# Seven block products in place of eight for three of eleven pairs of rows in the last output products of a two-layer decoder trunk

## The chip, the cores and the metric

The kernel runs on one core of one Trainium2 chip. The metric is the device time of one execution in microseconds; before the change the median of three runs is 2616.62 us.

## The reference

A decoder trunk of two layers on 256 tokens of width 2048, everything in fp32. Layer 0 mixes tokens by multi-scale retention, layer 1 by a short gated convolution; each layer then has a SwiGLU feed-forward part with 5632 inner rows. Every sub-layer is normed, scaled and shifted by columns that come from a conditioning vector `c` (the modulation), and its output is multiplied by a gate column and added to `x`. A final norm with a gain closes the trunk.

```python
def swiglu(h, w_in, w_out):
    a, b = jnp.split(h @ w_in, 2, axis=-1)
    return (jax.nn.silu(a) * b) @ w_out

for i in range(DEPTH):
    mod = (c_act @ w_mod[i] + b_mod[i])[:, None, :]
    sh1, sc1, g1, sh2, sc2, g2 = jnp.split(mod, 6, axis=-1)
    ...
    x = (x + g1 * y).astype(x.dtype)
    h = (rms_norm(x, norm2_g[i]) * (1.0 + sc2) + sh2).astype(x.dtype)
    x = (x + g2 * swiglu(h, ffn_w_in[i], ffn_w_out[i])).astype(x.dtype)
return rms_norm(x, final_g).astype(x.dtype)
```

## The kernel before

**Weights.** All weights lie in one array in the order of their use, cut into chunks of 128 x 2048 numbers (1 MB). `fetch` loads a chunk into one of three `raw` buffers from SP's queue. `prepare` works on half a chunk, a *piece* of 128 x 1024: ACT rounds it to `hi` (L311), VectorE subtracts to get the rest `lo` (L314). There are four buffers each of `hi` and `lo`. `take` hands out the block for the next matmul and sees to it that two more pieces are asked for (`AHEAD`). Activations are split in the same manner, and a product is the sum of three matmuls: hi with hi, hi with lo, lo with hi.

**Modulation.** Each column of the modulation is one load of 1 MB of `w_mod` into a `raw` buffer and one reduction on VectorE with `c` spread over 2048 columns (`cb`, L245), with a lowered priority. `paced` doles these out as weight blocks of 128 x 128 are used, after the table `plan_mod`; `needed` forces out the ones that a step cannot do without.

**The last layer's feed-forward part** goes in two halves of 22 inner rows (rows of 128). `swiglu_in` makes the 22 gate products of a half and splits each into `mid`. Beside the first half's, `turn` transposes `x` to one row for each token (`xt`). Then the output product: the moving operand is a weight block of 128 rows by 512 columns, the stationary one 128 tokens of `mid`, and the sum over 22 rows of each column block of 512 stands in two PSUM banks, one for each 128 tokens (`by_token`, L371 to L373). The four column blocks follow one another. `added` multiplies a sum by the gate (L1065) and adds it to `xt` (L1066); in the second half it also squares (L1069) and multiplies by the gain (L1071). For the last column block the final six rows (`TAIL_ROWS`) are done first for one half of the tokens, then for the other, so that `stored` can finish and store the first half meanwhile.

**Gate and gain.** `gate_stored` transposes the gate column to a row and stores it to DRAM, `spread` loads it back broadcast over 128 partitions into the space of `x` that is free by then, and the gain with it. Both are called within the first column block of the first half, before its rows 2 and 8 (`STORE_AT`, `LOAD_AT`).

TensorE's order is written out by hand; on VectorE, ACT and POOL a scheduler orders the instructions of this stage by priority. All loads and stores go through SP's queue, in order.

Of the kernel before, what the change touches and what calls it, by code (L numbers as in the profile page):

```python
# [17 lines left out]
P = 128  # L18
# [22 lines left out]
STORE_AT, LOAD_AT = 2, 8  # L41
# [14 lines left out]
class Group:  # L56


    def __init__(self, cols, width=P, ks=range(KT)):

        self.items = [c if isinstance(c, tuple) else (c, width) for c in cols]
        self.cols, self.ks = [c for c, _ in self.items], list(ks)
        self.n = sum(w for _, w in self.items) // P

# [67 lines left out]
LAST_OUT = [[Group([c], DV, ks=ks) for c in range(0, D, DV)] for ks in halves(DFF)]  # L132


def in_use_order():
# [10 lines left out]
    for layer in range(DEPTH):  # L146
# [5 lines left out]
        for part in range(2):  # L152
            for g in FFN_IN[part]:
                yield "ffn_w_in", layer, g
            for g in (LAST_OUT if layer == DEPTH - 1 else FFN_OUT)[part]:
                yield "ffn_w_out", layer, g


def laid_out(arrays):
# [4 lines left out]
    for key, i, g in in_use_order():  # L164
        for k in g.ks:
            for c, w in g.items:
                o = at % CHUNK
                out[at // CHUNK, :, o : o + w] = arrays[key][i, k * P : (k + 1) * P, c : c + w]
                at += w
# [18 lines left out]
def trunk(ctx: ExitStack, tc: tile.TileContext, x_in, c_in, pos_in, w_mod, cols_in, gain_in, tab_in, w_all, out):  # L188
# [20 lines left out]
    cb = const.tile([P, D], F32, tag="cb", name="cb")  # L209
    x4 = [const.tile([P, 4, S], F32, tag=f"x{i}", name=f"x{i}") for i in range(0, KT, 4)]  # L210
# [17 lines left out]
    nc.vector.memset(half, -0.5)  # L228

# [35 lines left out]
    plan_mod = [(early, 0), (1024, 18), (1984, 49), (5184, 9 * KT), (5888, n_mod)]  # L265
# [19 lines left out]
    order = [(g, k, c, w) for _, _, g in in_use_order() for k in g.ks for c, w in g.items]  # L285
    order.reverse()
    n_halves = w_all.shape[0] * CHUNK // HALF
    ready, taken_cols, raws, fetched, n_fetched = [], [0], [], [], [0]
# [7 lines left out]
    def prepare(between=None):  # L296
        n = prepared[0]
        if n == n_halves:
            return
        prepared[0] += 1  # L300
        i = n * HALF % CHUNK
        if i == 0:
# [5 lines left out]
        raw = raws[0][:, i : i + HALF]  # L308
        hi = wpool.tile([P, HALF], F32R, tag="hi", name=name("hi"))
        lo = wpool.tile([P, HALF], F32R, tag="lo", name=name("lo"))  # L310
# [4 lines left out]
        ready.append((hi, lo))  # L315

    prepared = [0]

    def take(group, k, col, width=P):

        assert order.pop() == (group, k, col, width)
        i = taken_cols[0] % HALF
        if i == 0:
            if ready and taken_cols[0]:
                ready.pop(0)
            while len(ready) < 1 + AHEAD * (units[0] >= first):
# [4 lines left out]
        taken_cols[0] += width  # L331
        return [t[:, i : i + width] for t in ready[0]]
# [32 lines left out]

    def by_token(banks, hi, lo, h, first, last, halves=range(2)):

        for t in halves:
            o = banks[t].rearrange("p a b -> p (a b)")
            ht = h[:, :, t * P : (t + 1) * P]  # L370
            nc.tensor.matmul(o, ht[:, 0, :], hi, start=first, stop=False)  # L371
            nc.tensor.matmul(o, ht[:, 0, :], lo, start=False, stop=False)  # L372
            nc.tensor.matmul(o, ht[:, 1, :], hi, start=False, stop=last)  # L373

    def packed(g, act, base=0, before=None, between=None, banks=None):
# [5 lines left out]
        for k in g.ks:  # L381
# [4 lines left out]
            for i, (c, width) in enumerate(g.items):  # L386
# [3 lines left out]
                if width == DV:  # L390
                    by_token(banks[at // 2 : at // 2 + 2], hi, lo, h, k == g.ks[0], k == g.ks[-1])
# [19 lines left out]
    def split(dst, src, at=slice(0, S)):  # L411
# [551 lines left out]
    def swiglu_in(layer, part, acc, mid, beside=()):  # L963

        pending, done, beside = [], 0, list(beside)
        for i, g in enumerate(FFN_IN[part]):
            pending += [sums(g)] if part or i else normed(acc, layer, 1, g)
            while len(pending) >= 2:
# [8 lines left out]
                split(mid[done], m)  # L977
# [55 lines left out]

    turns = [lambda t=t, c=c: turn(t, c) for c in range(4) for t in range(2)]


    flat = [v.rearrange("p a b -> p (a b)") for v in x4]
    gate_of = [at(flat[c // 2], c % 2) for c in range(4)]
    gain_of = [at(flat[2 + c // 2], c % 2) for c in range(4)]
# [10 lines left out]
    def spread():  # L1050
# [4 lines left out]
        for i in range(2):  # L1055
            o = slice(i * D // 2, (i + 1) * D // 2)
            nc.sync.dma_start(flat[2 + i], gain_in[:, o].broadcast_to([P, D // 2]))

# [98 lines left out]
```

## Time and profile before

| | |
|---|---|
| median of three runs | 2616.62 us (2616.34 to 2619.89) |
| the profiled execution | 2621.43 us, its span 2619.7 us |
| granted TensorE clock, mean | 0.999 |
| last layer's feed-forward part, first half: gate products, output product | 1882 to 2127 us, 2127 to 2247 us |
| second half: gate products, output product | 2247 to 2491 us, 2491 to 2611 us |
| HBM read | 685.08 MB, 262 GB/s over the span |

Times in the trace are microseconds from the start of the span; PE is TensorE's matmuls, PEld its weight loads, DVE is VectorE, ACT ScalarE, POOL GpSimd, SP the queue of loads and stores. "L314" is line 314 of the kernel. A group of instructions is written as line, engine, operation, output and inputs, shape and count, then busy time and the mean duration in ns, then the idle time ahead of it and what ended that. In a table by stretches each engine has its busy time and, in brackets, the number of its instructions; after them come the granted clock, the busy share of the DMA engines and GB/s. A row of the timeline has its start, its duration (of all, where several are merged), and then the same names.

### The profile page before, as it was taken

What the parts mean: (1) busy time and instruction counts of PE and PEld (TensorE: products, weight loads), DVE (VectorE), ACT (ScalarE), POOL (GpSimd) and SP (SyncE); (2) the same over time, 40 slices, a digit from 0 to 9 for tenths busy, and PEclk for the clock granted to TensorE, in tenths of its full rate; (3) what the DMA queues carried; (4) which work ended last, traced back from release to release, by engine and by line L of the source; (5) the groups of instructions that cost most, each with busy time, mean ns of one, the idle gap of its engine ahead of it and who ended that gap; (6) DMA issues with size and microseconds to landing.
All of it is one profiled execution on the core that took longest, in us unless ns stands there. A gap on an engine that the chain in (4) does not pass through costs nothing.

```text
span 2619.7 us, 37456 instructions
## 1 busy us (share of the span) xinstructions
PE 2587.4 (99%) x14867; PEld 2283.7 (87%) x14867; DVE 1982.7 (76%) x2490; ACT 1248.5 (48%) x1784; POOL 148.4 (6%) x232
## 2 busy tenths in 40 slices
PE   7999999999999999999999999999999999999998
PEld 6898889888899888888888898888998888888887
DVE  7988977887698887777777889888887765555554
ACT  5544543444456444344444454444564443444443
POOL 0000000110000001101100001100000000000000
PEclk9999999999999999999999999999999999999999
DMA  9976668877686887777777758777777775555554
GB/s 398 393 288 224 252 243 305 291 253 277 243 303 244 314 298 275 286 282 283 283 277 273 282 216 326 293 267 265 265 268 261 263 251 193 193 187 186 191 193 145
DMA packets 96834, 689.62 MB, mean 263 GB/s; under 512 B 10753, under 2 KB 12177, under 8 KB 13713
## 3 DMA queue, kind: packets, MB, share of 16 engines
q1 hardware_dynamic: 96658, 687.23, 71.1%
q8 instruction: 116, 1.90, 0.3%
q14 instruction: 60, 0.49, 0.0%
HBM read 685.08 MB, written 2.11 MB: 262 GB/s over the span
## 4 chain that ended last, share of the span: by engine, by line
PE 87%; DMA 6%; DVE 5%; issue 1%; ACT 1%; ACTq 0%; POOLq 0%; POOL 0%; DVEq 0%
PE bank L356 37%; PE bank L359 19%; PE bank L372 7%; PE bank L371 7%; PE bank L373 7%; DMA raw<-w_all 4%; DVE lo L314 2%; PE bank L398 2%; PE bank L397 2%; PE bank L396 2%; DMA raw<-w_mod 2%; PE bank L529 1%; PE bank L531 1%; PE bank L530 1%; DVE raw L657 1%
## 5 line engine op out<-in xcount | busy, mean ns | idle before, releaser
L314 DVE TENSOR_TENSOR lo<-raw,hi 128x1024 fp32r<-128x1024 f32 x912 | 1113.0, 1224 | 562.3 <-ACT hi L311 560.5
L311 ACT CAST hi<-raw 128x1024 fp32r<-128x1024 f32 x912 | 953.6, 1050 | 1084.1 <-PE bank L356 478.9
L356 PE MATMUL bank<-h,hi 128*128 128x512 f32 x3296 | 1144.2, 390 | 0.2 <-ACT hi L311 0.2
L359 PE MATMUL bank<-h,lo 128*128 128x256 f32 x3296 | 929.6, 282 | 1.3 <-DVE lo L314 1.3
L356 PEld LDWEIGHTS bank<-h,hi 128*128 128x128 f32 x3296 | 618.6, 188 | 129.7 <-ACT hi L311 0.5
L359 PEld LDWEIGHTS bank<-h,lo 128*128 128x128 f32 x3296 | 622.9, 189 | 2.0 <-DVE lo L314 1.9
L245 DVE SCALAR_TENSOR_TENSOR raw<-raw,cb 128x2048 f32<-128x2048 f32 x160 | 365.8, 2286 | 24.6 <-DMA raw<-w_mod 24.2
L356 PE MATMUL bank<-mid,hi 128*128 128x512 f32 x922 | 319.8, 390 | 0.0
L359 PE MATMUL bank<-mid,lo 128*128 128x256 f32 x922 | 260.1, 282 | 1.4 <-DVE lo L314 1.4
L356 PEld LDWEIGHTS bank<-mid,hi 128*128 128x128 f32 x922 | 173.1, 188 | 36.2
L371 PE MATMUL bank<-hi,h 128*128 128x512 f32 x512 | 201.4, 393 | 2.0 <-DVE rm L641 1.4
L372 PE MATMUL bank<-lo,h 128*128 128x512 f32 x512 | 200.1, 391 | 0.8 <-DVE lo L314 0.8
L373 PE MATMUL bank<-hi,h 128*128 128x512 f32 x512 | 199.4, 389 | 0.0
L359 PEld LDWEIGHTS bank<-mid,lo 128*128 128x128 f32 x922 | 174.3, 189 | 1.7 <-DVE lo L314 1.7
L356 PE MATMUL bank<-rm,hi 128*128 128x512 f32 x496 | 172.5, 390 | 0.0
L398 PE MATMUL bank<-h,lo 128*128 128x256 f32 x512 | 146.2, 285 | 5.4 <-DVE lo L314 5.4
L396 PE MATMUL bank<-h,hi 128*128 128x256 f32 x512 | 145.6, 284 | 3.3 <-ACT h L685 3.3
L397 PE MATMUL bank<-h,hi 128*128 128x256 f32 x512 | 145.5, 284 | 0.7 <-DVE h L686 0.7
L359 PE MATMUL bank<-rm,lo 128*128 128x256 f32 x496 | 139.8, 282 | 0.0
L371 PE MATMUL bank<-hi,mid 128*128 128x512 f32 x352 | 137.0, 389 | 0.0
L372 PE MATMUL bank<-lo,mid 128*128 128x512 f32 x352 | 136.9, 389 | 0.0
L373 PE MATMUL bank<-hi,mid 128*128 128x512 f32 x352 | 136.9, 389 | 0.0
(175 smaller groups left out, 2700.0 us busy)
## 6 DMA issues: line engine op xcount, KB each, us to landing
raw<-w_all SPq DMA_DIRECT2D x456, 1024.0 KB, 4.8
raw<-w_mod SPq DMA_DIRECT2D x192, 1024.0 KB, 5.1
x<-x_in SPq DMA_DIRECT2D x4, 512.0 KB, 5.5
out<-xt SPq DMA_DIRECT2D x4, 512.0 KB, 3.0
decay<-tab_in SPq DMA_DIRECT2D x8, 128.0 KB, 2.4
x<-gain_in SPq DMA_DIRECT2D x2, 512.0 KB, 6.8
x<-gate_row SPq DMA_DIRECT2D x2, 512.0 KB, 5.3
cols<-cols_in SPq DMA_DIRECT2D x1, 152.0 KB, 8.6
```

What stands on the lines that cost most here:

```text
L245: nc.vector.scalar_tensor_tensor(raw, raw, 1.0, cb, op0=ALU.mult, op1=ALU.mult, accum_out=total)
L311: nc.scalar.copy(hi, raw)
L314: nc.vector.tensor_tensor(lo, raw, hi.bitcast(F32), op=ALU.subtract)
L356: nc.tensor.matmul(pt, hi, h, start=fresh and k == g.ks[0], stop=False, skip_group_check=True)
L359: nc.tensor.matmul(pt[:, 1, :], lo, h[:, 0, :], start=False, stop=last and k == g.ks[-1], skip_group_check=True)
L371: nc.tensor.matmul(o, ht[:, 0, :], hi, start=first, stop=False)
L372: nc.tensor.matmul(o, ht[:, 0, :], lo, start=False, stop=False)
L373: nc.tensor.matmul(o, ht[:, 1, :], hi, start=False, stop=last)
L396: nc.tensor.matmul(pt, hi, h[:, 0, :], start=first, stop=False, skip_group_check=True)
L397: nc.tensor.matmul(pt, hi, h[:, 1, :], start=False, stop=False, skip_group_check=True)
L398: nc.tensor.matmul(pt, lo, h[:, 0, :], start=False, stop=last, skip_group_check=True)
L529: nc.tensor.matmul(pt, hi, high, start=k == 0, stop=False, skip_group_check=True)
```

## The change

For the pairs of rows 1, 4 and 7 (`SEVEN`) of the eleven pairs of a half, and for each pair of column blocks, the 2 x 2 block product (two token halves, two rows, two column blocks) is made of seven products by Strassen's method in Winograd's form.

- The weights of such a pair lie in one chunk, in the order B11, B12, B22, B21. `prepare` now makes five kinds of pieces from it or from ordinary chunks: B22 and B21; the differences T1 and T3 (a subtraction of 1024 columns into the space of `x`'s rows 8 to 11); B11 and T2 (a subtraction of 512 ahead of it); T4 (a subtraction of 512, and only 512 columns to split).
- `maker` stands in for `split` in `swiglu_in`: for these pairs it also makes the sums of the token blocks (four operations on 128 x 128) and splits them; they lie in the place of `cb`, for which all modulation has to be done before the last layer's feed-forward part.
- `last_output` works on two column blocks together, with all eight PSUM banks: four sums of its own and four for the products P1, P5, P6, P7. After the third such pair `mixed_sums` adds these up in 512-column operations; in the last column pair it also multiplies them by the gate and adds them to `xt` at once, elsewhere this is done at the column pair's end. The last column pair keeps the six rows of the tail apart.
- `plan_mod` ends at 5184 units (the start of the last feed-forward part) in place of 5888. While the output products run, three pieces are asked for ahead in place of two.
- `STORE_AT` and `LOAD_AT` are now counted in pairs, 0 and 2; the gain is loaded in the second half, in one load of 1 MB.

```diff
-STORE_AT, LOAD_AT = 2, 8
+SEVEN, BESIDE_CB = (1, 4, 7), 88
+STORE_AT, LOAD_AT = 0, 2
...
+class Seven:
+    n = 2 * DV // P
+    def __init__(self, cols, ks):
+        self.cols, self.ks = cols, list(ks)
+    def blocks(self):
+        (a, b), (i, j) = self.cols, self.ks
+        return [(i, a, DV), (i, b, DV), (j, b, DV), (j, a, DV)]
+    def uses(self):
+        return [(self, None, n, DV) for n in ("B22", "B21", "T1", "T3", "B11", "T2", "T4")]
...
-    plan_mod = [(early, 0), (1024, 18), (1984, 49), (5184, 9 * KT), (5888, n_mod)]
+    plan_mod = [(early, 0), (1024, 18), (1984, 49), (5184, n_mod)]
...
+        if piece == 2:
+            nc.vector.tensor_tensor(differences, whole[:, DV : 3 * DV], whole[:, : 2 * DV], op=ALU.subtract)
+        elif piece == 3:
+            raw = differences
+        elif piece == 4:
+            nc.vector.tensor_tensor(b[1], b[2], differences[:, :DV], op=ALU.subtract)
+        elif piece == 5:
+            nc.vector.tensor_tensor(b[3], b[3], b[1], op=ALU.subtract)
+            raw = b[3]
...
+    def maker(mid):
...
+            nc.vector.tensor_tensor(s3, a11, a21, op=ALU.subtract)
+            nc.vector.tensor_tensor(s1, a21, a22, op=ALU.add)
+            nc.vector.tensor_tensor(s2, s1, a11, op=ALU.subtract)
+            nc.vector.tensor_tensor(s4, a12, s2, op=ALU.subtract)
+            split(mid[i - 1][:, :, P:], s3)
+            split(tokens_sums[SEVEN.index(i // 2)], u[:, : 3 * P])
...
+    def sevens(g, act, base, ours, banks, first, last):
...
+        for use, x, (o, a, z) in zip(g.uses(), (s4, a12, s1, s3, a11, s2, a22), (
+            (ours[0, 1], False, False), (ours[0, 0], False, False), p5, p7, p1, p6, (ours[1, 0], False, False)
+        )):
+            thrice(o, x, take(*use), a, z)
...
+    def mixed_sums(banks, fold, c):
+        p1, p5, p6, p7 = banks
...
+        nc.scalar.copy(u1, p1)
+        nc.vector.tensor_tensor(u2, p6, u1, op=ALU.add)
+        nc.vector.tensor_tensor(u3, p7, u2, op=ALU.add)
+        nc.vector.tensor_tensor(u4, p5, u3, op=ALU.add)
+        nc.vector.tensor_tensor(u2, p5, u2, op=ALU.add)
+        out = {(0, 0): u1, (1, 0): u3, (1, 1): u4, (0, 1): u2}
+        if fold:
+            for (t, j), v in out.items():
+                gated(t, c + j, v, 0)
+        return out
...
+        for (t, j), pt in ours.items():
+            nc.vector.tensor_tensor(extra[t, j], pt, extra[t, j], op=ALU.add)
+        for (t, j), v in extra.items():
+            gated(t, c + j, v, MOD_PRIO)
...
     for part in range(2):
         mid = mids() if part else first_mid
-        swiglu_in(1, part, acc, mid, () if part else turns)
...
+        swiglu_in(1, part, acc, mid, () if part else turns, maker(mid))
+        ahead_now[0] = AHEAD + 1
+        for c, groups in enumerate(LAST_OUT[part]):
+            last_output(part, 2 * c, groups, mid, part * (FT // 2))
+        ahead_now[0] = AHEAD
```

More of the change, by code (lines that the diff above doesn't have):

```diff
@@ L154, in in_use_order @@
                 yield "ffn_w_in", layer, g
-            for g in (LAST_OUT if layer == DEPTH - 1 else FFN_OUT)[part]:
+            for g in sum(LAST_OUT[part], []) if layer == DEPTH - 1 else FFN_OUT[part]:
                 yield "ffn_w_out", layer, g
@@ L961, in sums, with swiglu_in @@
         return lambda dst=None: summed(pt, dst)
-    def swiglu_in(layer, part, acc, mid, beside=()):
+    def swiglu_in(layer, part, acc, mid, beside=(), made=split):
         pending, done, beside = [], 0, list(beside)
```

213 lines of the change are left out of this document (155 added, 58 removed).

## The prediction

> **What bounds the kernel now.** I read the page first, then the chain of waits over the last layer's feed-forward stage, then the busy time of each engine by stage.
>
> ```profile
> span 2619.7 us, 37456 instructions
> ...
> PE 2587.4 (99%) x14867; PEld 2283.7 (87%) x14867; DVE 1982.7 (76%) x2490; ACT 1248.5 (48%) x1784; POOL 148.4 (6%) x232
> ```
>
> ```profile
> by line: PE bank L356 40.2%; PE bank L359 21.3%; PE bank L372 10.6%; PE bank L373 10.6%; PE bank L371 10.6%; PE bank L531 1.4%; PE bank L529 1.4%; PE bank L530 1.4%; PE bank L1031 0.5%; ACT u L1069 0.2%; DVE xt L1066 0.2%; DVE u L1065 0.2%;
> ```
>
> ```profile
> core 0: us, PE busy (x) PEld busy (x) DVE busy (x) ACT busy (x) POOL busy (x), PEclk, DMA share, GB/s
> ...
> 1966.00:2127.00 161.00, 161.00 (x931) 142.75 (x930) 114.11 (x137) 77.66 (x116) 7.36 (x11) 1.00 0.72 264
> 2247.00:2491.00 244.00, 244.00 (x1409) 216.31 (x1408) 140.06 (x177) 117.22 (x175) 0.00 (x0) 1.00 0.54 190
> 2491.10:2610.60 119.50, 119.50 (x528) 98.64 (x526) 64.06 (x67) 49.17 (x59) 5.07 (x7) 1.00 0.46 162
> ```
>
> From 1880 us to the end the chain is TensorE alone but for the last microseconds (its rows L371 to L373 are the output products). The second half's output product runs 528 matmuls in 119.5 us without a gap, at a granted clock of 1.00: 226.3 ns each, start to start. VectorE is busy for 64 of these 119.5 us, the DMA engines for 46%. A matmul taken out here shortens the run by its pitch, as long as the pieces of weights stay ready.
>
> **The change part by part.**
>
> *Matmuls removed.* A pair of rows by a pair of column blocks took 8 block products of 3 matmuls; it takes 7. Three pairs of eleven, two column pairs, two halves: 12 times 3, so 36 matmuls, and the built programs differ by just that number. 36 x 0.2263 = **-8.15 us**. This is the whole of the gain that can come.
>
> The Trainium skill (TensorE: Matmul & The Clock Gate, Back-to-back issue gap) gives about 131 ns per matmul of 512 columns in a stream with weight loads, and 216 ns for one alone; the saving would be an estimated 4.7 or 7.8 us, and this trace's pitch disagrees with the first and lies near the second.
>
> *Work added per seven-product pair.* Price of VectorE's operations, at their pitch in a full queue:
>
> ```profile
> 2155.51 1.23 DVE L314 TENSOR_TENSOR lo<-raw,hi 128x1024 fp32r<-128x1024 f32 x1 [1.50 <-ACT hi L311]
> 2156.66 1.28 DVE L1065 TENSOR_TENSOR u<-bank,x 128x512 f32<-128x512 f32 x2
> 2157.85 1.28 DVE L1066 TENSOR_TENSOR xt<-xt,u 128x512 f32<-128x512 f32 x2
> 2159.05 1.22 DVE L314 TENSOR_TENSOR lo<-raw,hi 128x1024 fp32r<-128x1024 f32 x1
> ```
>
> ```profile
> L314 DVE TENSOR_TENSOR lo<-raw,hi 128x1024 fp32r<-128x1024 f32 x44 | 53.9, 1225 | 57.8 <-ACT hi L311 57.8
> L311 ACT CAST hi<-raw 128x1024 fp32r<-128x1024 f32 x44 | 46.4, 1054 | 72.6 <-PE bank L373 69.6 <-issue 1.5 <-PE bank L356 1.5
> ```
>
> Starts 2155.51 to 2156.66 give 1.15 us for 1024 columns; 2156.66 to 2159.05 give 0.60 for 512. A seven-product pair needs one difference and three splits of 1024 columns and three operations of 512: 4 x 1.15 + 3 x 0.60 = 6.4 us, against 21 x 0.2263 = 4.75 us on TensorE. An ordinary pair needs 2.3 against 5.43. Alone, such a pair would be bound by VectorE; over eleven pairs it is 3 x 6.4 + 8 x 2.3 = 37.6 against 57.7 us, so it hangs on the four hi/lo buffers. ACT may begin a piece when TensorE has left the piece four before it. Counted from the start of the ordinary pair ahead (its end 5.43, the seven's four pieces end at 6.8, 8.1, 9.5, 10.2): the seven's splits end about 0, 2.3, 5 and 6.7, each before its use at 5.43, 6.8, 8.1, 9.5. The tightest is the next ordinary piece: buffer free at 6.8, ACT 1.05, VectorE 1.15, ready at 9.1, used at 10.2. I cost these at **nothing**, with 1.1 us to spare; without that cover 12 x (6.4 - 4.75) = 20 us.
>
> *Sums of tokens* (the sums made beside the gate products): four 128x128 operations and one larger split per such pair. The trace has no 128x128 operation on VectorE; its neighbours are
>
> ```profile
> 2109.59 0.42 DVE L976 TENSOR_TENSOR m<-sum,silu 128x256 f32<-128x256 f32 x1
> ...
> 2613.02 0.21 DVE L1081 TENSOR_SCALAR rs<-total,sums 128x1 f32<-128x1 f32 x1 [0.79 <-ACT u L1069]
> ```
>
> so 0.21 to 0.42 each and, with the splits, 1.5 to 2.7 us for each of six pairs. Nearest is 128x256, so 2.7. They lie under TensorE in stages where VectorE has 47 of 161 and 104 of 244 us free: **nothing**; 16 us with no cover.
>
> *Sums of products and the fold.* Operations of 512 columns in the second half rise from 22 to 42 (4 sums twice, 4 drains, 16 for gate and addition, 8 and 6 as before). VectorE goes to about 64 + 6 x 4.1 + 20 x 0.6 = 101 us of 115, still below TensorE. At the change of column pair the eight PSUM banks are taken so that the first products go to banks long drained. But in the last column pair the built order puts sums, gates and additions together between two splits of weights. With the same zero: split of the second piece after the sevens ends at 10.5, a sum and the next split end at 12.3, then seven operations of 512 (16.5), a split (17.65), four of 512 (20.05), and the split that the last column block's second piece needs ends at 21.2. TensorE wants it after the 36 matmuls of the next column block, six of the last block's first piece and one more: 10.2 + 43 x 0.2263 = 19.9. What waits behind that split is the whole of the last 36 matmuls. **+1.3 us.** From 0 (if these ran at the 0.4 us of the nearest cheaper operation, 2609.76 to 2610.16 below) to 2.3 (if each took its full duration).
>
> The Trainium skill (VectorE: DVE Perf Modes, The TRN2 errata) gives (N+151)/0.96 ns for an fp32 addition: 691 ns at 512 columns and 1224 at 1024. The durations agree (0.68, 1.22), the pitch is shorter; by the rule this stall would be an estimated 2.4 us.
>
> *The end.* Now the first half of the tokens is finished while TensorE still works on the second:
>
> ```profile
> 2606.59 0.69 DVE L1065 TENSOR_TENSOR u<-bank,x 128x512 f32<-128x512 f32 x1 [4.49 <-PE bank L373]
> ...
> 2608.87 0.21 DVE L1081 TENSOR_SCALAR rs<-total,sums 128x1 f32<-128x1 f32 x1 [0.86 <-ACT u L1069]
> ...
> 2609.76 1.34 ACT L1088 ACTIVATE xt<-xt,rs 128x512 f32<-128x512 f32 x2 [0.99 <-POOL rs L1085]
> 2609.76 0.49 DVE L1092 TENSOR_SCALAR xt<-xt,rs 128x512 f32<-128x512 f32 x1 [0.67 <-POOL rs L1085]
> 2610.16 0.75 DVE L1090 SCALAR_TENSOR_TENSOR xt<-xt,rs,x 128x512 f32<-128x512 f32 x1
> 2610.82 0.68 DVE L1065 TENSOR_TENSOR u<-bank,x 128x512 f32<-128x512 f32 x1
> ...
> 2612.26 0.63 ACT L1069 ACTIVATE u<-xt 128x512 f32<-128x512 f32 x1 [1.17 <-DVE xt L1066]
> ...
> 2613.97 1.33 ACT L1088 ACTIVATE xt<-xt,rs 128x512 f32<-128x512 f32 x2 [0.98 <-POOL rs L1085]
> ```
>
> In the changed program's order the addition for the second half (which waits for the last matmul) stands on VectorE ahead of the first half's scalar (the row at 2608.87), and on ACT the first half's two scalings stand ahead of the second half's square. From the last matmul: 0.72 to the scalar, 0.89 to the scalings (2608.87 to 2609.76), 1.34 for them, then the square, 0.76 to its scalar (2612.26 to 2613.02) and 0.95 to the last scalings: 4.66 us, against 2613.97 - 2610.82 = 3.15, or 3.3 from the last matmul's end. **+1.4 us.** Bounds 0.9, if the wait on POOL is shorter, and 2.4, if the four stores, now closer together, add a microsecond.
>
> *Modulation moved.* The 16 reductions that ran beside the last layer's first gate products go ahead, into the stages before (144 there become 160).
>
> ```profile
> L245 DVE SCALAR_TENSOR_TENSOR raw<-raw,cb 128x2048 f32<-128x2048 f32 x160 | 365.8, 2286 | 24.6 <-DMA raw<-w_mod 24.2
> ```
>
> Each takes 2.29 us of VectorE, one of three raw buffers and 1 MB of loading on SP's queue, between two loads of weights. Where they leave, TensorE had no gap (161.00 of 161.00): no gain. Where they go:
>
> ```profile
> 861.20:916.80 55.60, 16.06 (x14) 1.00 0.85 313
> 916.80:972.40 55.60, 13.78 (x12) 1.00 0.82 297
> 1584.00:1639.60 55.60, 16.37 (x15) 1.00 0.89 336
> ```
>
> ```profile
> 861.20:916.80 55.60, 54.11 (x309) 47.27 (x308) 44.85 (x53) 25.74 (x40) 1.56 (x7) 1.00 0.85 313
> 916.80:972.40 55.60, 55.60 (x323) 49.27 (x322) 45.71 (x55) 28.20 (x42) 5.64 (x9) 1.00 0.82 297
> 1584.00:1639.60 55.60, 55.60 (x322) 49.28 (x321) 49.74 (x66) 24.69 (x33) 5.76 (x14) 1.00 0.89 336
> ```
>
> (The first three rows are L245 alone, two instructions a reduction.) Seven reductions in 55.6 us cost TensorE 1.5 us once and nothing once; six cost nothing. The order of load instructions in the built programs has seven reductions per ten weight loads (some 55 us) in three more such stretches, where they were four to six. **+1.5 us**, between 0 and 4.5.
>
> *Gate row, gain, banks.* The gate row is stored at the stage's start, and its two loads stand behind it:
>
> ```profile
> 2131.39 0.33 SPq L1048 DMA_DIRECT2D gate_row<-row  x1
> 2134.30 0.81 SPq L1054 DMA_DIRECT2D x<-gate_row  x2
> 2135.23 10.99 SPq L292 DMA_DIRECT2D raw<-w_all  x3
> ```
>
> 2.9 us lie from store to loads. The weight load queued behind them waits anyway for the first seven's buffer, some 7 us into the stage, and its pair is due 21 us in. The 1 MB of gain goes to the second half, past weight loads that are two pairs ahead of use, with the DMA engines at 46%. **Nothing**; if a load lands late, up to its time of about 5 us.
>
> *Sum:* -8.15 + 1.3 + 1.4 + 1.5 = **-3.95 us**. The profiled execution took 2621.43 us (span 2619.7 and 1.7 around it) and lies 4.8 above the median of the runs, 2616.62; the same difference on the median gives **2612.7 us**.
>
> **The rivals.**
>
> *All is hidden but the end's order.* Then -8.15 + 1.4 = -6.75: 2609.9 us. For it: VectorE's free time; a stretch with seven reductions and no loss. Against: the eleven small operations stand in the queue as counted.
>
> *The moved reductions make the raw buffers the bound* (slower). In the first and second layer loads then come late throughout. The new order has eleven stretches of ten weight loads with six or more reductions, where the old one has four; if all but the one that loses already lose 1.5 us each, 15 us: -8.15 + 2.7 + 15 = +9.6, 2626.2 us. It decides the sign from some 5.5 us of loss (four stretches). Against: the stretch from 916.8 us, six with no loss.
>
> *The sevens run at VectorE's pace* (slower): +20 us, so -8.15 + 2.7 + 1.5 + 20 = +16, 2632.7 us. It decides once a third of the 20 us shows. For it: 6.4 against 4.75. Against: the buffers, as counted.
>
> **How the numbers follow.** 0.2% (5.2 us) is about what a measurement of this kernel tells from no change. Forecast 0.52 (within 0.2%), all hidden 0.36 (faster), reductions 0.07 and sevens 0.05; of these two 0.11 is slower by over 0.2%, 0.01 within. Faster 0.36, same 0.53, slower 0.11. The range goes from 2608.0 (everything hidden and a shorter end) to 2619.0 (4.5 for the reductions and the upper bounds of the end, -8.15 + 2.3 + 2.4 + 4.5 = +1.05, and a little of the slower cases).
>
> **What would show it.** Output products shorter by 4.1 us each half (119.5 to about 115.4); a gap of 1 to 2 us on TensorE inside the last 10 us of matmuls, ended by a split of weights; 4.6 us from the last matmul to the last scalings; TensorE's busy time between 860 and 1900 us short by 1 to 4 us more than before. Gaps on TensorE at the seven-product pairs, or a loss of over 5 us before 1880 us, would prove the forecast wrong.

## The result and the profile after

The changed kernel takes 2613.47 us (median of 14 runs, 2610.95 to 2619.51) against 2619.19 us for the kernel before in the same comparison (14 runs, 2616.32 to 2622.01). The ratio is 0.998, with a 95% interval of 0.9972 to 0.9988: between 3 and 7 us faster. So the change is faster, but whether by more or by less than 0.2% (5.2 us), the limit that the forecast used, the interval leaves open. The profiled execution took 2613.33 us, its span 2611.6 us.

The first two lines of the page of the changed kernel answer to those shown of before:

```profile
span 2611.6 us, 37574 instructions
...
PE 2580.2 (99%) x14831; PEld 2278.1 (87%) x14831; DVE 2060.3 (79%) x2622; ACT 1271.9 (49%) x1824; POOL 131.6 (5%) x232
```

There are 36 matmuls fewer (14831 for 14867), 132 more operations on VectorE with 78 us more of its time, and the span is 8.1 us shorter. That is as much as all 36 matmuls are worth, which makes it look as if everything else had been hidden. It is not so. The span can be cut at landmarks that both kernels have: the sums of squares of three norms on TensorE (rows of the chain of waits), and the first and last matmuls of the stages of the last layer (rows of the timeline). The second column is another execution of the kernel before, unchanged (an experiment below); the last is the best version found.

| us from landmark to landmark | before, as shown | before, again | after | folded between (below) |
|---|---|---|---|---|
| start to first norm's sums | 784.90 | 784.36 | 784.52 | 783.28 |
| to second norm's sums | 737.05 | 734.74 | 734.74 | 734.74 |
| to third norm's sums | 359.24 | 358.27 | 358.73 | 358.38 |
| to first half's output product | 245.68 | 245.68 | 245.71 | 245.71 |
| first half's output product | 119.84 | 119.83 | 115.70 | 115.71 |
| second half's gate products | 244.07 | 244.07 | 244.08 | 244.07 |
| second half's output product, to the last matmul's end | 119.86 | 119.86 | 117.74 | 115.78 |
| from there to the end | 9.06 | 8.99 | 10.38 | 8.93 |
| span | 2619.7 | 2615.8 | 2611.6 | 2606.6 |

Three parts of the result are read from it. First, the first half's output product fell by 4.14 us, which is 18 matmuls at their pitch. Second, the second half's fell by only 2.12, and the end after it grew by 1.32. Third, up to the third norm's sums the two profiles differ by 3.2 us, 2.3 of them between the first and second norm, where the change only moved loads and reductions about. Against the second execution of before that part of the difference is gone: 1877.37 us up to the third norm's sums, against 1877.99 for the changed kernel.

The busy time of each engine over the two output products of the changed kernel:

```profile
2123.70:2239.40 115.70, 115.70 (x513) 95.80 (x511) 89.59 (x97) 57.28 (x61) 0.00 (x0) 1.00 0.58 208
...
2483.50:2601.20 117.70, 116.40 (x512) 95.28 (x510) 96.89 (x112) 58.17 (x71) 5.91 (x6) 1.00 0.48 174
```

The first number behind the length is TensorE: busy for all of the first half, 1.3 us short in the second. VectorE (the third) rose from 64 us of 119.5 to 97 of 117.7. The timeline of TensorE has most of the 1.3 us in one place:

```profile
2592.73 0.39 PE L435 MATMUL bank<-hi,mid 128*128 128x512 f32 x1
2594.35 0.50 PE L436 MATMUL bank<-lo,mid 128*128 128x512 f32 x1 [1.23 <-DVE lo L380]
2594.69 0.39 PE L437 MATMUL bank<-hi,mid 128*128 128x512 f32 x1
```

From one start to the next it is 0.23 us as a rule (the pitch), here once 1.62: a gap of 1.39 over the pitch, 8.5 us before the last matmul's end, ended by a split of weights (L380, line 314 of before). VectorE's timeline says what the split stood behind:

```profile
2584.20 1.22 DVE L380 TENSOR_TENSOR lo<-raw,hi 128x1024 fp32r<-128x1024 f32 x1
2585.33 0.68 DVE L1212 TENSOR_TENSOR x<-bank,u 128x512 f32<-128x512 f32 x1
...
2588.33 1.29 DVE L1171 TENSOR_TENSOR u<-u,x 128x512 f32<-128x512 f32 x2
2589.54 1.22 DVE L380 TENSOR_TENSOR lo<-raw,hi 128x1024 fp32r<-128x1024 f32 x1
2590.67 0.68 DVE L1172 TENSOR_TENSOR xt<-xt,x 128x512 f32<-128x512 f32 x1
...
2593.08 2.35 DVE L380 TENSOR_TENSOR lo<-raw,hi 128x1024 fp32r<-128x1024 f32 x2
```

Seven operations of the fold (L1212 to L1214 and four of L1171), a split, four more (L1172), and only then, at 2593.08 us, the split that TensorE waits for (the first of two shown as one row). It ends at about 2594.3, and the matmul starts at 2594.35.

### The profile page after: what moved, and what is told of

Same layout as the page of the kernel before. It is cut to its first block, busy times and chain, and to the rows that moved or that the text cites. A ratio compares the mean times of both kernels' runs of the same rounds, so it can differ in the third digit from the quotient of the medians.

```text
span 2611.6 us, 37574 instructions
## 1 busy us (share of the span) xinstructions
PE 2580.2 (99%) x14831; PEld 2278.1 (87%) x14831; DVE 2060.3 (79%) x2622; ACT 1271.9 (49%) x1824; POOL 131.6 (5%) x232
## 4 chain that ended last, share of the span: by engine, by line
PE 91%; DVE 4%; DMA 3%; issue 1%; ACT 1%; POOL 0%; ACTq 0%; POOLq 0%; DVEq 0%
PE bank L422 40%; PE bank L425 21%; PE bank L436 6%; PE bank L435 6%; PE bank L437 6%; DMA raw<-w_all 2%; PE bank L471 2%; PE bank L470 2%; PE bank L469 2%; DVE lo L380 1%; PE bank L602 1%; PE bank L604 1%; PE bank L603 1%; DMA raw<-w_mod 1%; DVE raw L730 1%
## 5 line engine op out<-in xcount | busy, mean ns | idle before, releaser
L380 DVE TENSOR_TENSOR lo<-raw,hi 128x1024 fp32r<-128x1024 f32 (+1 forms) x924 | 1117.6, 1215 | 461.7 <-ACT hi L377 458.2
L377 ACT CAST hi<-raw 128x1024 fp32r<-128x1024 f32 (+1 forms) x924 | 957.9, 1045 | 1012.8 <-PE bank L422 430.8
L436 PE MATMUL bank<-lo,mid 128*128 128x512 f32 x304 | 118.5, 390 | 1.3 <-DVE lo L380 1.2
L435 PE MATMUL bank<-hi,mid 128*128 128x512 f32 x304 | 118.4, 389 | 0.0
L437 PE MATMUL bank<-hi,mid 128*128 128x512 f32 x304 | 118.3, 389 | 0.0
```

Source lines behind the costliest of these rows:

```text
L377: nc.scalar.copy(hi, raw)
L380: nc.vector.tensor_tensor(lo, raw, hi.bitcast(F32), op=ALU.subtract)
L435: nc.tensor.matmul(o, hi, w_hi, start=first, stop=False)
L436: nc.tensor.matmul(o, hi, w_lo, start=False, stop=False)
L437: nc.tensor.matmul(o, lo, w_hi, start=False, stop=last)
```

## The experiments

All of them are in this table; the stage lengths are from one profiled execution each, the ratios from several timed runs of the kernel and of the kernel before.

| run | first half's output | second half's output | last matmul to last scalings | second output's start to the end | first to second norm | ratio to before, 95% |
|---|---|---|---|---|---|---|
| before | 119.84 | 119.86 | 3.33 | 128.92 | 737.05 | |
| before, a second and a third time | 119.83, 119.83 | 119.86, 119.86 | 3.33, 3.33 | 128.85, 128.83 | 734.74, 734.74 | |
| after | 115.70 | 117.74 | 4.82 | 128.12 | 734.74 | 0.998 (0.9972 to 0.9988) |
| earlier plan alone | 119.84 | 119.86 | 3.33 | 128.88 | 736.87 | 1.000 (0.9991 to 1.0009) |
| end ordered as before | 115.71 | 117.31 | 5.03 | 127.81 | 734.74 | 0.998 (0.9971 to 0.9989) |
| pairs 1, 4, 6 | 115.71 | 116.00 | 3.64 | 125.18 | 734.74 | 0.9978 (0.9968 to 0.9989) |
| pairs 4, 7 | 117.06 | 118.69 | 4.82 | 129.03 | 734.83 | |
| 88 unused columns alone | 119.83 | 119.86 | 3.32 | 128.82 | 734.92 | 0.9999 (0.999 to 1.0008) |
| after, without them | 116.25 | 117.86 | 4.82 | 128.18 | 734.74 | 0.9986 (0.9977 to 0.9995) |
| pairs 1, 2, 3 | 117.79 | 117.86 | 3.39 | 126.73 | 734.74 | |
| plan much earlier | 119.84 | 119.86 | 3.32 | 128.84 | 738.06 | |
| pairs 1, 3, 5 | 115.71 | 117.14 | 3.39 | 126.06 | 734.74 | 0.9976 (0.9965 to 0.9986) |
| pairs 1, 3, 5, fold in between | 115.71 | 115.78 | 3.39 | 124.71 | 734.74 | 0.9971 (0.9962 to 0.998) |

### The moved modulation: the earlier plan alone

The kernel before with one line of the change.

```diff
-    plan_mod = [(early, 0), (1024, 18), (1984, 49), (5184, 9 * KT), (5888, n_mod)]
+    plan_mod = [(early, 0), (1024, 18), (1984, 49), (5184, n_mod)]
```

> The kernel before with the changed plan of the modulation alone (all 160 reductions done by 5184 units). Landmarks are the norm sums on TensorE: in the profile before they lie at 784.9, 1521.95 and 1881.19 us, in the changed kernel at 784.5, 1519.3 and 1878.0; so the first two stretches took 737.1 and 359.2 us before, 734.7 and 358.7 after. Theory A (the plan itself brings the gain ahead of the last feed-forward part, since it changes which loads stand between weight loads around 860 us): the first stretch takes 734.5 to 735.5 us, the whole time is 2 to 3 us below the kernel before. Theory B (the gain there is chance of one execution, the plan does nothing): 737 us, the time within 1 us. Theory C (my prediction: the moved reductions cost 1.5 us): 738.5 us, the time 1.5 us above.

2618.30 us (11 runs) against 2618.53 (24 runs), a ratio of 1.000. From the first to the second norm it took 736.87 us, as the shown profile of before did. So the times show no cost of the earlier plan, though an interval of 2.4 us to either side would not tell the predicted 1.5 us from nothing; the stage lengths below do. Nor does the plan alone make this stretch 2.3 us shorter in every execution.

### The end: its order put back

VectorE and ACT take the last column block's operations in the order in which they are written, as they came out before the change.

```diff
-                for t in range(2):
+                by_hand = {mybir.EngineType.DVE, mybir.EngineType.Activation}
+                with tc.manual_schedule(engines=by_hand) if tail else ExitStack():
+                    for t in range(2):
...
```

> The changed kernel with VectorE's and ACT's order written out by hand behind the last column block, so that the first half of the tokens is finished ahead of the second half's addition, as in the kernel before. Theory (the new order at the end costs 1.4 us): from the last matmul's end to the last scalings 3.3 us in place of 4.8; from the second half's last gate product to the end of the span 126.7 us in place of 128.1; the gap of 1.2 us on TensorE stays. Rival (the end is set by the stores): the scalings come earlier, but the span's end stays within 0.3 us of 128.1.

It gained nothing at the end: 5.03 us from the last matmul to the last scalings, where the change has 4.82 and before 3.33. (The 0.3 us by which the stretch from the second output's start to the end is shorter, 127.81 for 128.12, come from a small delay at 2551.5 us, spoken of below, that this run does not have.) The timeline of this run shows why (VectorE and ACT, the last matmul ends at 2599.2 us):

```profile
2596.33 1.28 DVE L1183 TENSOR_TENSOR xt<-xt,last_gain 128x512 f32<-128x512 f32 x2
2597.53 0.69 DVE L1178 TENSOR_TENSOR xt<-xt,u 128x512 f32<-128x512 f32 x1
...
2599.96 1.34 ACT L1231 ACTIVATE xt<-xt,rs 128x512 f32<-128x512 f32 x2 [0.98 <-POOL rs L1228]
...
2601.02 0.69 DVE L1177 TENSOR_TENSOR u<-bank,x 128x512 f32<-128x512 f32 x1
```

The first half's last addition (L1178) comes at 2597.53 because two multiplications by the gain (L1183) of the column block before, themselves late behind the fold, stand ahead of it. So the first half's scalings start 0.8 us after the last matmul; before the change they started 0.9 us ahead of it (2609.76 against 2610.64). The second half's first operation, which could start at 2599.2, starts at 2601.02 behind them. So the order alone does not make the cost: VectorE is late when the end begins, and either order then costs 1.5 to 1.7 us.

### The fold earlier: pairs 1, 4 and 6

```diff
-SEVEN, BESIDE_CB = (1, 4, 7), 88
+SEVEN, BESIDE_CB = (1, 4, 6), 88
```

> The changed kernel with pairs 1, 4 and 6 in place of 1, 4 and 7, so that the sums of products and the fold come one ordinary pair (5.4 us) earlier. The end's order turns back as a side effect. Theory (the eleven operations of 512 columns ahead of the late split make the gap, and the buffers carry two seven-product pairs with one ordinary pair between them): no gap on TensorE in the second half's output product, which takes 115.6 to 116.0 us in place of 117.7; with the end back at 3.3 us the stretch from the last gate product to the end takes 125.2 to 125.8 us in place of 128.1. Rival (the gap comes from the smaller slack behind the seven-product pairs, with one ordinary pair between there is more of it): gaps of 1 us or more at pairs 5 to 7 in each column pair, no gain.

The large gap is gone (116.00 us for the second half's output product; two delays of 0.1 us are left), and the last scalings come 3.64 us after the last matmul. From the second output product's start to the end it takes 125.18 us in place of 128.12: the same work, in the same order (seven operations of the fold, a split, four more) but begun 5.4 us of matmuls earlier, is nearly hidden. The end comes free with it. As expected, the scheduler has turned its order back here by itself: the first half's scalings start at 2599.19 us, 0.6 us ahead of the last matmul's end.

### What a matmul is worth: pairs 4 and 7

```diff
-SEVEN, BESIDE_CB = (1, 4, 7), 88
+SEVEN, BESIDE_CB = (4, 7), 88
```

> The changed kernel with pairs 4 and 7 alone by seven products. Theory (a matmul taken out is worth its pitch): 24 matmuls saved in place of 36; first half's output product 115.7 + 2.7 = 118.4 us, second half from its last gate product to the end 128.1 + 2.7 = 130.8 us, less up to 0.4 if the small loss of the third column pair went with pair 1. Rival (VectorE's work limits the sevens, so that each is worth less): the first half's grows by less than 2 us.

Twelve matmuls more in all, so six for each half: 6 x 0.2263 = 1.36 us. The expectation counted the twelve for each half; that was a slip in the arithmetic. Measured: 1.36 us in the first half (117.06 - 115.70) and 0.95 in the second. The second half's is lower because a delay of some 0.4 us that the change has in its second half, at 2551.5 us behind pair 1, is not there when pair 1 is an ordinary one. The worth of a matmul is its pitch, to within 0.01 us for the six in the first half. The gap near the end stayed (1.40 us over the pitch), as the fold's place is the same.

### Where the early 2.3 us came from

All runs of the changed kernel so far had 734.7 to 734.8 us between the first two norms, and before and the earlier plan had 737. The difference between them that was tried next was the place of the buffers in SBUF: the change puts 88 unused columns behind `cb`. Two runs cross these: the kernel before with the columns, and the changed one without.

```diff
     cb = const.tile([P, D], F32, tag="cb", name="cb")
+    const.tile([P, 88], F32, tag="beside_cb", name="beside_cb")
```

> The kernel before with one line of the change alone: 88 unused columns of fp32 (352 bytes in each partition) behind cb, which push every later SBUF buffer up by 352 bytes; no instruction is added or moved. Theory (places in SBUF): the buffers' new places are what took 2.1 to 2.3 us out of the stretch from 784 to 1522 us in every variant of the changed kernel; then the distance between the first and second norm's sums falls from 737.0 to 734.8 us here too, loads at 840 to 930 us land in 5 to 6 us in place of 7.1, the output products stay at 119.85 us each, and the run is 2 to 3 us shorter than before. Rival (the gain belongs to something else in the changed program, such as the earlier plan together with another order in the last stage): 736.9 to 737.1 us between these sums, loads as before, time within 1 us of before.

> The changed kernel without those 88 unused columns; nothing else differs. Theory (places in SBUF): 736.9 us between the first and second norm's sums, a loss of about 1.2 us of TensorE in 880 to 930 us comes back, and the span grows from 2611.6 to about 2614; the output products stay at 115.7 and 117.7 us. Rival: 734.7 us, span 2611 to 2612.5.

Before with the columns had 734.92 us, as the theory of places said, and yet its time was that of before (0.9999). After without them kept 734.74, against the theory. So the theory fell, and a simpler one was tried: the kernel before itself, unchanged, twice more.

> The kernel before, unchanged, once more. Theory (scatter: the 2.2 us between the first and second norm's sums, 737.05 in the profile of before and 734.74 in that of after, are a loss that some executions have and others do not, whatever the kernel): the distance lies anywhere between 734.7 and 737.1 us, and in at least one of this run and the next it is under 735.5. Rival (it belongs to the program of before): 736.8 to 737.1 us in both.

> The kernel before, unchanged, a third time. Theory and rival as for the run ahead of it: 734.7 to 737.1 us with at least one of the two under 735.5, against 736.8 to 737.1 us in both.

Both had 734.74 us. Here are the landmarks in the chains of waits, first of the profile of before that was shown, then of its second execution:

```profile
784.90 0.79 PE bank L434 x8
1521.95 0.79 PE bank L434 x8
```

```profile
784.36 0.79 PE bank L434 x8
1519.10 0.79 PE bank L434 x8
```

737.05 and 734.74 us, from one kernel. In the first, the chain leaves TensorE from 835 to 902 us and runs over loads; two of its pieces:

```profile
882.57 7.84 DMA raw<-w_mod
...
892.86 6.57 DMA raw<-w_all
```

The medians from issue to landing between 860 and 930 us, in the first execution and then in the second:

```profile
raw<-w_all SPq DMA_DIRECT2D x13, 1024.0 KB, 6.8
raw<-w_mod SPq DMA_DIRECT2D x9, 1024.0 KB, 6.4
```

```profile
raw<-w_all SPq DMA_DIRECT2D x12, 1024.0 KB, 5.5
raw<-w_mod SPq DMA_DIRECT2D x9, 1024.0 KB, 5.2
```

In the first execution the same loads land over a microsecond later, and the delay reaches TensorE. Late loads are not enough for that: in the run with pairs 4 and 7 the medians were 6.4 and 5.9 us, and it lost nothing there. Busy time in that stretch, in the second execution (the first has 54.11 of 55.60, in the prediction):

```profile
861.20:916.80 55.60, 55.60 (x322) 49.28 (x321) 48.63 (x56) 27.64 (x42) 1.57 (x7) 1.00 0.91 339
```

So the loss is one that the kernel before has in some executions and not in others. Why loads land later in some of them isn't settled. Of all fourteen profiled executions two lost over 1 us from 861 to 917 us, the first of before and that of the earlier plan; two more of before, two of its variants and eight with seven-product pairs did not. (One of these variants, the much earlier plan, lost time elsewhere between the two norms; see below.) The change, then, needs no part in it; whether it makes the loss rarer, these few can't say.

### Seven-product pairs next to each other

```diff
-SEVEN, BESIDE_CB = (1, 4, 7), 88
+SEVEN, BESIDE_CB = (1, 2, 3), 88
```

> The changed kernel with the seven-product pairs next to each other, pairs 1, 2 and 3 of a column pair in place of 1, 4 and 7; the same 36 matmuls less, and the last one is folded in early, so that the gap of 1.2 us near the end should be gone. Theory (the four hi/lo buffers hide each such pair's 6.4 us of VectorE against 4.75 of TensorE because the pairs between them give the lead back): three in a row need 19.2 us of VectorE in 14.3 of TensorE, some 5 us more than it, of which the buffers' lead covers about 3.5; a stall of 1 to 2 us in each of four column pairs, first half's output product 118 to 120 us, second half's 118 to 120. Rival (they hide wherever they stand): 115.7 and about 116.0 us. Rival (they run at VectorE's pace): 5 us lost in each column pair, 125 us each.

117.79 and 117.86 us: 2.1 us more than with the pairs apart, so a good 1 us in each column pair, at the low end of what was expected. (The expectation's 5 us by 6.4 and 4.75 a pair, less the lead, gives 1 where the lead is worth 4.) TensorE, and the split that it waits for, on the timeline of this run:

```profile
2141.76 1.22 DVE L380 TENSOR_TENSOR lo<-x,hi 128x1024 fp32r<-128x1024 f32 x1
2142.56 0.40 PE L435 MATMUL bank<-hi,sums_of_tokens 128*128 128x512 f32 x1
2143.03 0.50 PE L436 MATMUL bank<-lo,sums_of_tokens 128*128 128x512 f32 x1
2143.37 0.40 PE L437 MATMUL bank<-hi,sums_of_tokens 128*128 128x512 f32 x1
```

The split ends at 2142.98, the matmul that needs `lo` starts at 2143.03 in place of 2142.79. The same repeats at the next pieces: here VectorE sets the pace. In the first half, with two ordinary pairs between (the change), or one (pairs 1, 3 and 5, below), nothing of it is left. The lead that the four buffers give is real and used up within three such pairs in a row.

### Seven reductions a stretch: the plan much earlier

The kernel before; all reductions are to be done by 4160 units in place of 5888.

```diff
-    plan_mod = [(early, 0), (1024, 18), (1984, 49), (5184, 9 * KT), (5888, n_mod)]
+    plan_mod = [(early, 0), (1024, 18), (1984, 49), (4160, n_mod)]
```

> The kernel before with all 160 reductions of the modulation planned to be done by 4160 units of the order of work in place of 5888, so seven to nine of them per 55.6 us from some 850 to 1600 us. The rule behind the prediction's term and its slower rival (a stretch of 55.6 us with seven reductions loses 1.5 us of TensorE): 12 or more such stretches, 15 to 25 us lost, span 2635 to 2645. Theory (only the stretches at 860 to 930 us and 1800 us, where the loads are late for another reason, lose): 0 to 4 us lost, span 2619 to 2624.

The span was 2622.3 us. First the reductions alone in three of the stretches (two instructions and 2.29 us a reduction), then all engines in the same three:

```profile
1062.00:1118.00 56.00, 17.61 (x15) 1.00 0.88 322
1118.00:1173.00 55.00, 16.32 (x16) 1.00 0.91 342
1451.00:1507.00 56.00, 13.89 (x14) 1.00 0.86 305
```

```profile
1062.00:1118.00 56.00, 55.00 (x315) 48.13 (x314) 47.49 (x51) 21.16 (x21) 1.62 (x8) 1.00 0.88 322
1118.00:1173.00 55.00, 55.00 (x319) 48.76 (x318) 45.97 (x52) 22.67 (x26) 3.47 (x8) 1.00 0.91 342
1451.00:1507.00 56.00, 54.89 (x315) 48.15 (x314) 47.96 (x62) 25.16 (x34) 1.33 (x7) 1.00 0.86 305
```

By their busy time, eleven stretches from 840 to 1674 us hold seven reductions or eight. One of them lost 1.0 us (1062 to 1118), ten nothing; two more losses, 1.11 us (1451 to 1507) and 1.26 us (1674 to 1729), lie in stretches with six. All in all it is 3.4 us, not 15 to 25. The rule that such a stretch loses 1.5 us is wrong by a wide margin, and with it the slower rival that was built on it; the number of reductions in a stretch doesn't tell which one loses.

### The fold: its amount or its run

First the pairs 1, 3 and 5, so that the fold comes earlier still.

```diff
-SEVEN, BESIDE_CB = (1, 4, 7), 88
+SEVEN, BESIDE_CB = (1, 3, 5), 88
```

> The changed kernel with the seven-product pairs at 1, 3 and 5, so one ordinary pair between two of them and the fold two pairs earlier than in the change. Theory (an ordinary pair gives the lead back: seven and ordinary together need 6.4 + 2.3 = 8.7 us of VectorE against 10.2 of TensorE, so the pairs next to each other were the cause of the stalls at 1, 2 and 3; and the earlier the fold, the less is left on VectorE at the end): no stall at the pairs, first half's output product 115.7 us, second half's 115.7 to 115.9, 3.3 to 3.5 us from the last matmul to the last scalings, 124.5 to 125.0 us from the second output product's start to the end (after: 128.1, pairs 1, 4 and 6: 125.2); 3 to 4 us faster than the change, ratio to before about 0.997. Rival (one pair between them isn't enough): 0.3 to 1 us of gaps at the second and third such pair in each column pair, first half's output product 116.5 to 117.8 us.

The first half was as expected, 115.71 us with no delay at the pairs, and so were the last scalings (3.39). The second half was a miss: 117.14 us, with a gap again. Its timeline, VectorE and TensorE:

```profile
2579.49 0.68 DVE L1212 TENSOR_TENSOR x<-bank,u 128x512 f32<-128x512 f32 x1
...
2585.94 0.39 PE L435 MATMUL bank<-hi,mid 128*128 128x512 f32 x1
2586.11 4.62 DVE L380 TENSOR_TENSOR lo<-raw,hi 128x1024 fp32r<-128x1024 f32 x4
2587.38 0.50 PE L436 MATMUL bank<-lo,mid 128*128 128x512 f32 x1 [1.05 <-DVE lo L380]
```

The scheduler has put the fold's operations in one run here: eleven, from 2579.49 to 2586.11 us, with no split among them. (The next expectation speaks of ten; the timeline has eleven.) The first of the four splits that follow comes too late. So an earlier fold isn't enough, and its place is not all that counts: pairs 1, 4 and 6, with one split among the eleven operations, lost 0.2 us in all. Here the order is the suspect, eleven operations without a split. The last run keeps these pairs and only lowers the priority of the fold's multiplications and additions:

```diff
-                gated(t, c + j, v, 0)
+                gated(t, c + j, v, 4 * MOD_PRIO)
```

> The kernel with seven-product pairs at 1, 3 and 5, and the fold's multiplications and additions at a lower priority; nothing is added or taken away. In its built order VectorE never has more than three operations of 512 columns between two splits of weights in the fold, where the run before had ten in a row. Theory (the stall near the end is the fold's run of operations without a split between them; with pairs 1, 3 and 5 it was ten operations, 6.6 us, and TensorE lost 1.2 us): no gap there, second half's output product 115.7 to 115.9 us in place of 117.1, 3.3 to 3.5 us from the last matmul to the last scalings, 124.6 to 125.0 us from its start to the end, about 1.3 us better than the run before, ratio to before about 0.997. Rival (the stall is the sheer amount of VectorE's work after the third such pair, in whatever order): a gap of about 1.2 us stays, 117 us, and 126 us to the end.

VectorE's timeline over the same part of the fold:

```profile
2581.75 0.68 DVE L1171 TENSOR_TENSOR u<-u,x 128x512 f32<-128x512 f32 x1
2582.47 1.23 DVE L380 TENSOR_TENSOR lo<-raw,hi 128x1024 fp32r<-128x1024 f32 x1
2583.61 1.29 DVE L1172 TENSOR_TENSOR xt<-xt,x 128x512 f32<-128x512 f32 x2
2584.82 0.69 DVE L1172 TENSOR_TENSOR xt<-xt,u 128x512 f32<-128x512 f32 x1
2585.42 1.22 DVE L380 TENSOR_TENSOR lo<-raw,hi 128x1024 fp32r<-128x1024 f32 x1
```

Two or three operations, then a split, and TensorE has no gap: 115.78 us, 3.39 us to the last scalings, 124.71 us to the end. That is all 18 matmuls of the second half, as in the first. Median 2610.62 us (11 runs) against 2618.92, a ratio of 0.9971 (0.9962 to 0.998). It is the fastest version found; its interval overlaps with those of pairs 1, 4, 6 and of the change, so that it beats them rests on the stage lengths of one execution each and not on the times.

## Why the prediction was right or wrong

The forecast was 2612.7 us, 3.95 below before. The measured ratio puts the change at 3 to 7 us, 5.2 in the middle. That 2612.7 lies only 0.8 us from the measured 2613.47 is partly luck: the forecast started from a median of 2616.62 for before, which came out as 2619.19 in the comparison, and its sum was 1 to 2 us short. Step by step:

- *36 matmuls, -8.15 us.* Right. The first half shows it bare (4.14 us for 18, against 18 x 0.2263 = 4.07), the run with pairs 4 and 7 from the other side (1.36 for six). The Trainium skill (TensorE: Matmul & The Clock Gate, Back-to-back issue gap), with its 131 ns in a stream, would give an estimated 0.8 us for those six; the measurement decides against it here.
- *The seven-product pairs' splits cost nothing.* Right, and for the reason given: pairs 1, 2 and 3 in a row lose 1 us a column pair, pairs with ordinary ones between them nothing, but for the small delay named in the next point. The rival in which they run at VectorE's pace would have shown 5 us for each of the four column pairs, 20 in all.
- *Sums of tokens, sums of products, gate row, gain: nothing.* Right as far as the stage lengths go: the second half's gate products take 244.08 us for 244.07, and the first half's output product is shorter by all that its 18 matmuls are worth. One small delay was not foreseen: 0.34 us at 2551.5 us, at the very piece that the prediction called the tightest (the ordinary one behind the first such pair). VectorE and TensorE there, in the changed kernel:

```profile
2549.47 0.68 DVE L1297 TENSOR_TENSOR xt<-xt,last_gain 128x512 f32<-128x512 f32 x1
2550.08 0.68 DVE L1172 TENSOR_TENSOR xt<-xt,x 128x512 f32<-128x512 f32 x1
2550.68 2.35 DVE L380 TENSOR_TENSOR lo<-raw,hi 128x1024 fp32r<-128x1024 f32 x2
...
2551.49 0.39 PE L435 MATMUL bank<-hi,mid 128*128 128x512 f32 x1
2551.95 0.50 PE L436 MATMUL bank<-lo,mid 128*128 128x512 f32 x1
```

In the second half's last column pair the drains, gates and gains of the column pair before stand among the splits there and use up the 1.1 us: the split ends at 2551.90, the matmul starts at 2551.95 in place of 2551.72.
- *The fold before a late split, +1.3 us.* Right in place, cause and size: 1.39 us, behind eleven operations with one split among them. With pairs 1, 3 and 5 the last run shows that it was the order of the operations, and not their amount, that cost 1.2 us; for the change's own pairs, which fold latest, no run alters the order alone, and the run with pairs 1, 4 and 6 shows that there the place counts too. By the Trainium skill's duration for an fp32 addition (VectorE: DVE Perf Modes, The TRN2 errata) it was an estimated 2.4 us; that duration agrees with the rows (0.68 us), but in a full queue the next operation starts after 0.60.
- *The order at the end, +1.4 us.* Right in size (4.82 - 3.33 = 1.49) and in the sequence of the rows:

```profile
2601.26 0.69 DVE L1177 TENSOR_TENSOR u<-bank,x 128x512 f32<-128x512 f32 x1 [1.02 <-PE bank L437]
...
2603.11 1.33 ACT L1231 ACTIVATE xt<-xt,rs 128x512 f32<-128x512 f32 x2 [2.12 <-POOL rs L1228]
2604.36 0.61 ACT L1181 ACTIVATE u<-xt 128x512 f32<-128x512 f32 x1
...
2606.04 1.33 ACT L1231 ACTIVATE xt<-xt,rs 128x512 f32<-128x512 f32 x2 [0.98 <-POOL rs L1228]
```

These are, on the timeline of the changed kernel, the second half's first operation, the first half's scalings, the second half's square and its scalings. But the order that was named as the cause is not enough of one: with the order of before the end is no shorter (5.03). The first half is late because VectorE still works off the fold; with the fold earlier or spread out, the end takes 3.39 to 3.64 us. In all these runs the scheduler also put the first half's scalings ahead of the second half's addition again, so what the new order would cost with VectorE on time is not shown.
- *The moved modulation, +1.5 us.* Wrong: the step that failed is "Seven reductions in 55.6 us cost TensorE 1.5 us once and nothing once". It took a loss that stood in one execution for the price of seven reductions. Two more executions of before have no loss in that stretch, all eight executions of kernels with seven-product pairs, which have the moved plan, took 734.74 to 734.83 us there, as before does without the loss, and eleven crowded stretches of the much earlier plan lost 1.0 us together, where the rule gives 16.5. The earlier plan alone takes the same time as before (1.000). Zero belongs in its place.

With these, the sum is -8.15 + 1.39 + 1.49 + 0.34 = -4.9 us; the two output products and the end, measured, give -4.14 - 2.12 + 1.32 = -4.94. So the forecast was 1 us short: 1.5 for a term that should have been nothing, in part made up by 0.34 that it left out. The profiled spans differ by 8.1 us; the 3.2 of it ahead of the last stage is scatter between executions, as the second execution of before shows. "All hidden but the end's order" (-6.75) would have needed TensorE without the gap at 2592.73 us, which is there. Of the two slower rivals, the one of the reductions was ruled out by the much earlier plan, and the one of VectorE's pace by the change's own first half.

Of the signs named in advance, the first half's length, the gap in the last 10 us of matmuls and the length of the end all came as described; the fourth, 1 to 4 us more lost between 860 and 1900 us, did not: TensorE lost 2.0 us less there (busy for 1039.09 of 1040 us, against 1037.10 in the profile of before).

## What to carry to other kernels

When work is to hide on an engine that also feeds the bottleneck, count not only its total but also its place and the runs in its queue without the feeding operation: with pairs 1, 3 and 5 the same fold cost 1.2 us in one order and nothing in another, and one priority decided it. Where several things are late at the end, restoring an order did nothing here while the queue ahead of it was still full. And before a difference between two profiles is explained, profile one of the two kernels a second time: a loss of 2.3 us that seemed to belong to the old kernel was not there when it ran again.

## What the hardware showed that was not expected

- One program, three profiled executions: 737.05, 734.74 and 734.74 us over the same stretch, at a mean granted clock of 0.998 or 0.999; loads of 1 MB had a median of 6.8 and 5.5 us from issue to landing between 860 and 930 us in the first two.
- A wait on TensorE costs more than its length: the matmul behind each gap takes 0.34 us to the next start in place of 0.23 (2594.35 to 2594.69, 2143.03 to 2143.37), so the many gaps of 0.24 us with adjacent pairs cost 0.35 each.
- Without the 88 unused columns the first half's output product took 116.25 us in place of 115.70, with no gap: single starts lie 0.24 us apart in place of 0.23. The twelve matmuls of `lo` with the sums of tokens in the place of `cb` have a mean of 396 ns against 389. The starts fall behind by about 0.13 us in each of pairs 1 and 4, whose sums stand in that place, in both column pairs, and not in pair 7, whose sums stand elsewhere. So the place of an operand in SBUF makes a small difference here, by this one execution; by what means stays open.

```profile
L435 PE MATMUL bank<-lo,in_cb 128*128 128x512 f32 x12 | 4.8, 396 | 0.0
```
